# Query and key score stacks: high and low parts made for both heads at once, the other row halves moved by DMA

## The chip, the cores and the metric

The kernel runs on one core of a Trainium2 chip. The metric is the device time of one execution in microseconds. A core has TensorE (PE; PEld is its weight load), VectorE (DVE), ScalarE (ACT), GpSimd (POOL) and SyncE (SP), which issues this kernel's DMAs from one queue, in order.

## The reference, cut to what matters

Two decoder layers run one after the other on 1024 positions of width 1024, in float32. Layer 0 mixes tokens by differential attention (8 heads of two 64-wide queries and keys, with a rotary embedding on 16 of the 64), layer 1 by forgetting attention (16 heads of 64). Each is followed by a layer norm and a gated MLP with a causal convolution.

```
q, k, v = jnp.split(x @ w_qkv, 3, axis=-1)
q = apply_rotary(q.reshape(B, S, H, 2, d), cos, sin, PARTIAL_ROT)...
s = jnp.einsum('bhcqd,bhckd->bhcqk', qb, k) * scale
p = masked_softmax(s, causal_mask(start, Q_BLOCK, S))
a = (p[:, :, 0] - lam * p[:, :, 1]).astype(v.dtype)
o = jnp.einsum('bhqk,bhkd->bqhd', a, v)
...
s = (jnp.einsum('bhqd,bhkd->bhqk', qb, k).astype(jnp.float32) * scale
     + cb[..., :, None] - c[..., None, :])
```

## The kernel before, in words

Float32 products are made of parts. `split` (L84 to L91) makes a high part in fp32r on ScalarE (L87) and the rest, the low part, on VectorE (L89, or L91 where a scale is applied). `mm3` (L98 to L100) multiplies high by high, low by high and high by low.

Sixteen head halves (layer 0) or heads (layer 1) are worked on in 8 pairs. A pair's projections are transposed: 128 rows are the features, 64 of each head, and 1024 columns are positions, made in two halves `c` of 512. For the scores each head has a stack of 128 rows. A query stack holds the high part in one half of its rows and the low part in the other: stack a has head 0's high part in rows 0 to 63 and its low part below, stack b head 1's high part in rows 64 to 127 and its low part above. A key stack holds the high part twice, and a third tile holds the low parts of both heads' keys. `scores` (L475 to L491) multiplies the stacks (L489), adds the query's high part, copied by GpSimd into `qz` (L482), times the keys' low part (L490), and the mask (L491).

`split_q` makes a site of 64 rows twice: two high and two low parts for a pair's half. `split_k` makes, for each head, a high part, a low part and a copy of the high part on ScalarE (L275). In layer 1 `result` (L409) calls them on the projection in PSUM. In layer 0 the projection is copied to a tile by L414, the rotary comes between, and `halves` (L420) calls them on the tile. The rotary is `gather` (L428: twelve small DMAs for a half, L437 and L439), `turn` (three VectorE operations, L446 to L448, and four DMAs back, L452).

`project` makes the next pair's projections in steps of a few matmuls, which are put between the attention jobs of the pair at work; `after` puts the eviction, the gathers, the turn and the halves a set number of steps behind the matmuls (D_EV, D_ROT, D_CUT). Within these, a scheduler sets the order of instructions on each engine. A softmax row block goes: scores on TensorE, maximum (L510), exponential (L513, ScalarE), reciprocal (L516), division (L518) or the difference of the two maps (L523), transposes on TensorE (L1304), their high and low parts `pt` (L87, L89), products with V. V is transposed by L458 and its parts are `q<-m` of 128 x 512. Weights are fetched on SP (L107, tag `wst`, 2 buffers, which the second map's exponential also takes) and split into `wh` and `wl`.

Of the kernel before, what the change touches and what calls it, by code (L numbers as in the profile page):

```python
# [9 lines left out]
F32 = mybir.dt.float32  # L10
F32R = mybir.dt.float32r
BF16 = mybir.dt.bfloat16
I32 = mybir.dt.int32
AF = mybir.ActivationFunctionType
# [5 lines left out]
P = 128  # L20
# [6 lines left out]
DH = 64  # L27
# [27 lines left out]
class Trunk:  # L55
# [205 lines left out]
    def qtile(self, par):  # L261
        return self.qp.tile([P, 1024], F32R, tag=f"q{par}", name=self.nm("q"))

    def split_q(self, par, src, scale, sl):

        for st, r in zip(par, (0, 64)):
            self.split(st[r:r + 64, sl], st[64 - r:128 - r, sl], src[r:r + 64, :], scale)

    def split_k(self, par, src, sl):

        a, b, lo = par
        for st, r in ((a, 0), (b, 64)):
            s = src[r:r + 64, :]
            self.split(st[r:r + 64, sl], lo[r:r + 64, sl], s)
            self.nc.scalar.activation(st[64 - r:128 - r, sl], s, AF.Copy)  # L275


    def after(self, n, fn, *args):
# [131 lines left out]
    def result(self, l, s, c, ps, dst, t):  # L410

        sl = slice(c * 512, c * 512 + 512)
        if dst is not None:
            self.nc.scalar.activation(dst[:, sl], ps, AF.Copy, scale=DH ** -0.5 if s == 0 else 1.0)  # L414
        elif s == 0:
            self.split_q(t[:2], ps, -DH ** -0.5, sl)
        else:
            self.split_k(t[2:5], ps, sl)

    def halves(self, dst, t, c, j):  # L420

        sl = slice(c * 512, c * 512 + 512)
        if j == 0:
            self.split_q(t[:2], dst[0][:, sl], None, sl)
        else:
            self.split_k(t[2:5], dst[1][:, sl], sl)

# [1082 lines left out]
```

## Time and profile before

| | us |
|---|---|
| three runs | 2513.72, 2516.26 (median), 2519.29 |
| profiled execution | 2511.37 |
| its span | 2509.6 |
| TensorE busy in the span | 2445.9 |
| VectorE busy | 1956.6 |
| ScalarE busy | 1336.5 |
| attention of layer 0, pairs 0 to 7 | about 45 to 500 |
| attention of layer 1 | about 1297 to 1740 |

Times in the trace count from the start of the span. Columns of a timeline are the start, the duration, the engine, the line, the operation, output and input, and in brackets the engine's idle time before it with what ended it. The duration of a matmul is modelled and pipelined, so that starts, not durations, tell how far apart matmuls are.

### The profile page before, as it was taken

Reading aid. Unit: us, or ns where it says so; the run is one execution under the profiler, and the core shown is the slowest. Engines: PE = TensorE matmul, PEld = TensorE weight load, DVE = VectorE, ACT = ScalarE, POOL = GpSimd, SP = SyncE. Lnnn points to the kernel's source line nnn. Section 1 sums busy time; section 2 is a strip of 40 time slices with the busy share of each in tenths; the row PEclk is TensorE's granted clock in tenths of the full one; section 3 lists DMA queues with packets and bytes.
Section 4 is the critical chain, followed back from the end, with each engine's and each line's share of the span. In section 5 each row is a group of like instructions: output and inputs, shape, how many; then the busy total and the mean of one; then the engine's idle time right before and its main releaser. Section 6 shows DMA issues by size and latency. Waiting matters only on the chain.

```text
span 2509.6 us, 33808 instructions
## 1 busy us (share of the span) xinstructions
PE 2445.9 (97%) x12059; PEld 2017.6 (80%) x12059; DVE 1956.6 (78%) x3669; ACT 1336.5 (53%) x2519; POOL 140.1 (6%) x322
## 2 busy tenths in 40 slices
PE   8999999999999999999999999999999999999997
PEld 6888777787888888788778888888878888888786
DVE  6787777989876677787868888888888667677867
ACT  5666666656544444444545666656465444444444
POOL 2001101101000000000101000000010000000001
PEclk9999999999999999999999999999999999999999
DMA  4111111422222223864411111114222222228743
GB/s 153 39 57 56 47 47 48 175 93 92 93 82 95 76 76 132 312 199 155 148 54 51 51 51 51 51 60 160 84 85 101 84 76 81 96 97 286 241 138 140
DMA packets 101865, 264.32 MB, mean 105 GB/s; under 512 B 15008, under 2 KB 22560, under 8 KB 101696
## 3 DMA queue, kind: packets, MB, share of 16 engines
q1 hardware_dynamic: 101184, 261.31, 30.5%
q8 instruction: 94, 1.54, 0.3%
q0 software_dynamic: 512, 0.85, 0.1%
q14 instruction: 75, 0.61, 0.1%
HBM read 196.70 MB, written 59.11 MB: 102 GB/s over the span
## 4 chain that ended last, share of the span: by engine, by line
PE 49%; DVE 5%; DMA 2%; ACT 1%; issue 1%; SPq 0%; POOL 0%; POOLq 0%; DVEq 0%; ACTq 0%
PE m L98 11%; PE m L100 11%; PE m L99 11%; PE s L100 3%; PE s L98 3%; PE s L99 3%; PE m L1304 2%; PE m L1329 1%; PE m L1330 1%; PE s L490 1%; PE s L489 1%; DMA ha<-ad 1%; DVE wo L89 1%; DVE wl L89 0%; DVE s L635 0%
## 5 line engine op out<-in xcount | busy, mean ns | idle before, releaser
L98 PE MATMUL m<-xh,wh 128*128 128x512 f32 x768 | 322.3, 420 | 9.1 <-ACT xh L87 8.8
L100 PE MATMUL m<-xh,wl 128*128 128x512 f32 x768 | 304.2, 396 | 0.0
L99 PE MATMUL m<-xl,wh 128*128 128x512 f32 x768 | 302.2, 393 | 0.4 <-DVE xl L89 0.4
L98 PE MATMUL m<-xh,wo 128*128 128x512 f32 x656 | 255.2, 389 | 0.0
L100 PE MATMUL m<-xh,wo 128*128 128x512 f32 x656 | 255.2, 389 | 0.0
L99 PE MATMUL m<-xl,wo 128*128 128x512 f32 x656 | 255.2, 389 | 0.0
L87 ACT ACTIVATE wo<-wg 128x512 fp32r<-128x512 f32 x168 | 106.4, 633 | 225.6 <-PE m L100 218.6
L87 ACT ACTIVATE pt<-m 128x512 fp32r<-128x512 f32 (+1 forms) x240 | 128.4, 552 | 121.1 <-PE m L1304 83.6
L98 PE MATMUL m<-q,wo 128*128 128x512 f32 x472 | 184.1, 390 | 0.0
L99 PE MATMUL m<-q,wo 128*128 128x512 f32 x472 | 183.8, 389 | 0.0
L100 PE MATMUL m<-q,wo 128*128 128x512 f32 x472 | 183.7, 389 | 0.0
L98 PEld LDWEIGHTS m<-xh,wh 128*128 128x128 f32 x768 | 145.7, 190 | 32.4 <-ACT xh L87 8.8
L100 PEld LDWEIGHTS m<-xh,wl 128*128 128x128 f32 x768 | 144.8, 188 | 31.5 <-DVE wl L89 0.6
L89 DVE TENSOR_TENSOR pt<-m,pt 128x512 fp32r<-128x512 f32 (+1 forms) x240 | 149.0, 632 | 22.5 <-ACT pt L87 19.8
L99 PEld LDWEIGHTS m<-xl,wh 128*128 128x128 f32 x768 | 145.7, 190 | 23.6 <-DVE xl L89 0.9
L87 ACT ACTIVATE wo<-t 128x512 fp32r<-128x512 f32 x132 | 82.8, 627 | 144.7 <-PE m L100 133.3
L89 DVE TENSOR_TENSOR wo<-wg,wo 128x512 fp32r<-128x512 f32 x168 | 115.4, 688 | 38.8 <-ACT wo L87 37.9
L482 POOL CAST qz<-q 64x128 fp32r<-64x128 f32 x256 | 93.3, 365 | 911.2 <-PE s L491 831.4
L98 PEld LDWEIGHTS m<-xh,wo 128*128 128x128 f32 x656 | 123.1, 188 | 25.7 <-ACT p L1037 0.2
L100 PEld LDWEIGHTS m<-xh,wo 128*128 128x128 f32 x656 | 123.1, 188 | 25.6
L99 PEld LDWEIGHTS m<-xl,wo 128*128 128x128 f32 x656 | 123.2, 188 | 25.4
L87 ACT ACTIVATE oa<-ha 128x512 fp32r<-128x512 f32 x108 | 67.4, 628 | 127.4 <-PE s L100 61.1
(319 smaller groups left out, 6363.5 us busy)
## 6 DMA issues: line engine op xcount, KB each, us to landing
wst<-in_w SPq DMA_DIRECT2D x46, 512.0 KB, 3.3
t<-in_wi SPq DMA_DIRECT2D x44, 512.0 KB, 4.4
ad<-t SPq DMA_DIRECT2D x44, 512.0 KB, 3.4
ha<-ad SPq DMA_DIRECT2D x88, 256.0 KB, 5.4
wg<-in_wi SPq DMA_DIRECT2D x42, 512.0 KB, 3.3
pt<-in_wd SPq DMA_DIRECT2D x34, 512.0 KB, 3.5
wb<-in_wd SPq DMA_DIRECT2D x42, 256.0 KB, 3.0
wst<-in_wo SPq DMA_DIRECT2D x16, 512.0 KB, 3.3
```

The costliest lines, as they stand in the source:

```text
L87: nc.scalar.activation(hi, src, AF.Copy, scale=1.0 if scale is None else scale)
L89: nc.vector.tensor_tensor(lo, src, hi.bitcast(F32), op=ALU.subtract)
L98: mm(out, wh, xh, start=start, stop=False)
L99: mm(out, wh, xl, start=False, stop=False)
L100: mm(out, wl, xh, start=False, stop=stop)
L482: nc.gpsimd.tensor_copy(qz[r:r + 64, :], q[r:r + 64, qt * P:qt * P + P])
L489: nc.tensor.matmul(sb[:, ks], q[:, qt * P:qt * P + P], kd[:, ks], start=True, stop=False)
L490: nc.tensor.matmul(sb[:, ks], qz, kl[:, ks], start=False, stop=not last)
L1304: nc.tensor.transpose(tb[:, w:w + P], self.pts[q][:, kt * P:kt * P + P], k.ident)
L1329: mm(o, self.v[0][:, vs], h, start=first, stop=False)
L1330: mm(o, self.v[0][:, vs], l, start=False, stop=last)
```

## The change

`split_q` and `split_k` work on all 128 rows, so that there is one high part and one low part for both heads. The halves of rows that then stand in the wrong stack are moved by `move`: three DMAs of 64 x 512 (128 KB) on SP for a query and three for a key, at 32 sites each. For a query: the high part of head 1 to stack b, the low part of head 1 to b's upper rows, then the low part of head 0 over the rows of a that held head 1's high part (which waits for the first move). For a key: the high part of head 1 to b, twice, then the high part of head 0 over a's lower rows (which waits for both). The low part of a query is written over the source tile in layer 0, and into a new tile `ql` (tag `t`) in layer 1. Lines behind the edit move by 4 or 6: L414 is L418, L437 to L439 are L443 to L445, L452 is L458, L458 is L464, L510 to L523 are L516 to L529, L1304 is L1310; the moves are L266.

```
+    def move(self, *pairs):
+        for dst, src in pairs:
+            self.nc.sync.dma_start(dst.bitcast(F32), src.bitcast(F32))
+
+    def split_q(self, par, src, scale, sl, lo):
+        a, b = par[0][:, sl], par[1][:, sl]
+        self.split(a, lo, src, scale)
+        self.move((b[64:], a[64:]), (b[:64], lo[64:]), (a[64:], lo[:64]))
...
-        for st, r in zip(par, (0, 64)):
-            self.split(st[r:r + 64, sl], st[64 - r:128 - r, sl], src[r:r + 64, :], scale)
...
-        a, b, lo = par
-        for st, r in ((a, 0), (b, 64)):
-            s = src[r:r + 64, :]
-            self.split(st[r:r + 64, sl], lo[r:r + 64, sl], s)
-            self.nc.scalar.activation(st[64 - r:128 - r, sl], s, AF.Copy)
+        a, b = par[0][:, sl], par[1][:, sl]
+        self.split(a, par[2][:, sl], src)
+        self.move((b[64:], a[64:]), (b[:64], a[64:]), (a[64:], a[:64]))
...
         elif s == 0:
-            self.split_q(t[:2], ps, -DH ** -0.5, sl)
+            if c == 0:
+                self.qlo = self.tp.tile([P, 1024], F32R, tag="t", name=self.nm("ql"))
+            self.split_q(t[:2], ps, -DH ** -0.5, sl, self.qlo[:, sl])
...
         if j == 0:
-            self.split_q(t[:2], dst[0][:, sl], None, sl)
+            self.split_q(t[:2], dst[0][:, sl], None, sl, dst[0][:, sl].bitcast(F32R))
```

The scheduler puts the instructions into a new order around this. On SP, at the start of pair 0 (t_144 and t_145 are its query and key, t_382 the rotary's tile, q_137 and q_138 the query stacks, q_139 and q_140 the key stacks), there stood before, from the last gathers of the second half on:

```order
L437 DMA t_382<-t_145 32x256
L439 DMA t_382<-t_145 16x256 x2
L107 DMA wst_562<-in_w 128x1024
L564 DMA bf<-in_bf 16x1
L568 DMA tri<-in_tri 128x128
L452 DMA t_144<-t_382 32x256 x2
L452 DMA t_145<-t_382 32x256 x2
L107 DMA wst_673<-in_w 128x1024
```

and now, from the last moves of the first half on:

```order
L266 DMA q_140<-q_139 64x512
L266 DMA q_137<-t_144 64x512
L445 DMA t_382<-t_144 16x256
L443 DMA t_382<-t_145 32x256
L266 DMA q_139<-q_139 64x512
L445 DMA t_382<-t_145 16x256 x2
L443 DMA t_382<-t_145 32x256
L445 DMA t_382<-t_145 16x256 x2
L107 DMA wst_562<-in_w 128x1024
L570 DMA bf<-in_bf 16x1
L574 DMA tri<-in_tri 128x128
L458 DMA t_144<-t_382 32x256 x2
```

So the first half's moves stand among the gathers of the second half, and the rotary's way back (L458, before L452) behind them all.

On ScalarE, in the second half of a middle pair (the one at 278 us; q_2469 to q_2472 are the next pair's stacks, pt_3161 a transposed probability), there stood before:

```order
L87 ACTIVATE q_2469<-t_2679 64x512
L87 ACTIVATE q_2470<-t_2679 64x512
L87 ACTIVATE q_2471<-t_2781 64x512
L87 ACTIVATE pt_3161<-m_3111 128x384
L275 ACTIVATE q_2471<-t_2781 64x512
L513 ACTIVATE wst_3167,ls_3093<-s_3086,nm_3092 128x1024
```

and now:

```order
L552 ACTIVATE sq_2967<-sq_2967 128x256
L87 ACTIVATE q_2469<-t_2679 128x512
L87 ACTIVATE pt_3161<-m_3111 128x384
L87 ACTIVATE q_2471<-t_2781 128x512
L519 ACTIVATE wst_3167,ls_3093<-s_3086,nm_3092 128x1024
```

The high part of `pt` stood behind the key's half and stands ahead of it now.

On VectorE, at the boundary of pair 0 and pair 1 (q_564 and q_565 are pair 1's query stacks, q_568 the low part of its keys), there stood before:

```order
L89 TENSOR_TENSOR pt_1148<-m_1109,pt_1148 128x384
L89 TENSOR_TENSOR q_565<-t_672,q_565 64x512
L89 TENSOR_TENSOR q_568<-t_760,q_566 64x512
L510 TENSOR_REDUCE nm_1139<-s_1135 128x1
L516 RECIPROCAL rs_1189<-ls_1091 128x1
L89 TENSOR_TENSOR q_568<-t_760,q_567 64x512
L522 TENSOR_TENSOR rs_1189<-rs_1189,nlam 128x1
L516 RECIPROCAL rs_1217<-ls_1140 128x1
L523 SCALAR_TENSOR_TENSOR p_1107<-wst_1154,rs_1189,p_1107 128x1024
```

and now:

```order
L89 TENSOR_TENSOR pt_1148<-m_1109,pt_1148 128x384
L557 SCALAR_TENSOR_TENSOR of_747<-sq_960,of_747 128x256
L522 RECIPROCAL rs_1190<-ls_1091 128x1
L89 TENSOR_TENSOR q_568<-t_760,q_566 128x512
L528 TENSOR_TENSOR rs_1190<-rs_1190,nlam 128x1
L516 TENSOR_REDUCE nm_1139<-s_1135 128x1
L529 SCALAR_TENSOR_TENSOR p_1107<-wst_1154,rs_1190,p_1107 128x1024
```

One low part stands between `pt` and the difference of the maps, where three stood.

## Rows read from the trace of the kernel before

**Rows 1.** The page: busy time of each engine
```profile
PE 2445.9 (97%) x12059; PEld 2017.6 (80%) x12059; DVE 1956.6 (78%) x3669; ACT 1336.5 (53%) x2519; POOL 140.1 (6%) x322
```

**Rows 2.** Windows: length, busy time of each engine, granted clock, DMA share, GB/s
```profile
60.00:500.00 440.00, 423.26 (x2318) 350.25 (x2318) 355.57 (x720) 288.58 (x617) 43.84 (x116) 1.00 0.20 66
1310.00:1740.00 430.00, 423.84 (x2490) 354.68 (x2489) 348.34 (x841) 261.14 (x553) 37.64 (x108) 1.00 0.19 64
```

**Rows 3.** TensorE's waits, 60 to 500 us: line, releaser, total, times, longest
```profile
PE m L458 <- DVE pt L89: 10.8, 6, 2.4
...
PE m L1304 <- DVE p L523: 1.6, 1, 1.6
```

**Rows 4.** TensorE's waits, 1310 to 1740 us
```profile
PE m L1304 <- DVE q L91: 1.2, 6, 0.2
```

**Rows 5.** Timeline of TensorE at the start of pair 0
```profile
49.21 0.39 PE L489 MATMUL s<-q,q 128*128 128x256 f32 x1 [0.97 <-ACT p L513]
...
51.98 0.39 PE L100 MATMUL m<-xh,wl 128*128 128x512 f32 x1
52.21 0.40 PE L98 MATMUL m<-xh,wh 128*128 128x512 f32 x1
53.96 0.39 PE L489 MATMUL s<-q,q 128*128 128x256 f32 x1 [1.35 <-ACT wst L513]
...
57.85 0.50 PE L1304 MATMUL m<-ident,p 128*128 128x128 f32 x3
```

**Rows 6.** Groups by line and shape: count, busy us, mean ns, idle before
```profile
L89 DVE TENSOR_TENSOR q<-t,q 64x512 fp32r<-64x512 f32 x64 | 44.0, 688 | 2.1 <-ACT q L87 0.4
L87 ACT ACTIVATE q<-t 64x512 fp32r<-64x512 f32 x64 | 40.1, 627 | 3.8 <-DMA t<-t 2.7
...
L89 DVE TENSOR_TENSOR xl<-t,xh 128x512 fp32r<-128x512 f32 x32 | 21.3, 682 | 1.5 <-ACT xh L87 1.5
...
L87 ACT ACTIVATE xh<-t 128x512 fp32r<-128x512 f32 x32 | 18.7, 628 | 4.6 <-DMA t<-od 4.6
```

**Rows 7.** DMA issues: count, KB of each, median us from issue to landing
```profile
wst<-in_w SPq DMA_DIRECT2D x46, 512.0 KB, 3.3
...
t<-t SPq DMA_DIRECT2D x128, 32.0 KB, 1.8
...
out<-acc SPq DMA_DIRECT2D x3, 128.0 KB, 1.9
```

**Rows 8.** Timeline of SP's queue: issue of the rotary's way back, pair 0
```profile
46.44 2.41 SPq L452 DMA_DIRECT2D t<-t  x4
```

**Rows 9.** Timeline of VectorE at the boundary of pairs 0 and 1
```profile
101.06 1.40 DVE L89 TENSOR_TENSOR q<-t,q 64x512 fp32r<-64x512 f32 x2
...
102.76 0.81 DVE L89 TENSOR_TENSOR q<-t,q 64x512 fp32r<-64x512 f32 x1
...
103.80 1.28 DVE L523 SCALAR_TENSOR_TENSOR p<-wst,rs,p 128x1024 f32<-128x1024 f32 x1
```

**Rows 10.** Timelines of ScalarE, VectorE and TensorE around 278 us
```profile
274.87 1.28 ACT L87 ACTIVATE q<-t 64x512 fp32r<-64x512 f32 x2
277.03 0.63 ACT L87 ACTIVATE q<-t 64x512 fp32r<-64x512 f32 x1 [0.89 <-DMA t<-t]
...
275.85 1.22 DVE L510 TENSOR_REDUCE nm<-s 128x1 f32<-128x1024 f32 x1
278.07 0.56 DVE L89 TENSOR_TENSOR pt<-m,pt 128x384 fp32r<-128x384 f32 x1 [1.00 <-ACT pt L87]
...
278.68 0.66 PE L458 MATMUL m<-ident,t 128*128 128x128 f32 x4 [2.01 <-DVE pt L89]
```

**Rows 11.** Timeline of VectorE in the pairs at 217 and 400 us
```profile
216.10 1.22 DVE L510 TENSOR_REDUCE nm<-s 128x1 f32<-128x1024 f32 x1
217.46 0.56 DVE L89 TENSOR_TENSOR pt<-m,pt 128x384 fp32r<-128x384 f32 x1
...
400.30 0.56 DVE L89 TENSOR_TENSOR pt<-m,pt 128x384 fp32r<-128x384 f32 x1 [1.20 <-ACT pt L87]
```

More of the change, by code (lines that the diff above doesn't have):

```diff
@@ L262, in qtile @@
         return self.qp.tile([P, 1024], F32R, tag=f"q{par}", name=self.nm("q"))
-    def split_q(self, par, src, scale, sl):
-        for st, r in zip(par, (0, 64)):
-            self.split(st[r:r + 64, sl], st[64 - r:128 - r, sl], src[r:r + 64, :], scale)
-    def split_k(self, par, src, sl):
-        a, b, lo = par
-        for st, r in ((a, 0), (b, 64)):
-            s = src[r:r + 64, :]
-            self.split(st[r:r + 64, sl], lo[r:r + 64, sl], s)
-            self.nc.scalar.activation(st[64 - r:128 - r, sl], s, AF.Copy)
+    def move(self, *pairs):
[5 more added lines that the diff above has]
+        self.move((b[64:], a[64:]), (b[:64], lo[64:]), (a[64:], lo[:64]))
+    def split_k(self, par, src, sl):
+        a, b = par[0][:, sl], par[1][:, sl]
+        self.split(a, par[2][:, sl], src)
+        self.move((b[64:], a[64:]), (b[:64], a[64:]), (a[64:], a[:64]))
     def after(self, n, fn, *args):
```

## The prediction

> **What bounds the kernel now.** I read the page first, then the windows of the two attention stretches, then TensorE's waits in them, then the timelines of the few waits that are left. On the page TensorE is busy for 97% of the span [rows 1]; no other engine is the bound, and ScalarE and VectorE matter only where TensorE waits for them. The change touches the two attention stretches. There TensorE is idle for 440.00 - 423.26 = 16.7 us in layer 0 and 430.00 - 423.84 = 6.2 us in layer 1 [rows 2], at full clock in both. So about 23 us is all that a lighter ScalarE and VectorE could win, out of some 2516.
>
> The waits say where that is [rows 3, 4]. Six times 1.8 us on average (10.8 in all) TensorE's transposes of V (L458) wait for the low part of a transposed probability, `pt`. Once, for 1.6 us, transposes of probabilities (L1304) wait for VectorE's L523. In layer 1 it is six times 0.2 us behind the low part of a query (L91). Before these windows, at the start of the first pair, scores wait 0.97 and 1.35 us for exponentials [rows 5]. Everything else is TensorE's own work, which the change leaves as it is.
>
> **What the split costs.** An operation of 64 rows takes as long as one of 128: the low part of 64 x 512 takes 688 ns, of 128 x 512 682; the high part 627 and 628 [rows 6]. So in layer 0 VectorE's 64 low parts of 44.0 us become 32 of 21.8, and ScalarE's 64 high parts of 40.1 us, with 32 copies of the same size beside them, become 32 of 20.1. Layer 1 has as many sites. These are large cuts, and nearly all of it is cover: TensorE waits for neither engine except at the places above. The work goes, the time doesn't, unless one of those waits ends earlier.
>
> **What the moves cost.** Each of the 64 sites issues three transfers of 128 KB on SP: 192 more, 25 MB. None like them is in the trace. From below, a 32 KB transfer between the same kind of tiles lands in 1.8 us; from above, 512 KB of weights land in 3.3; the nearest row is a 128 KB store with 1.9, and I take that [rows 7]. Issuing holds SP for 2.41 / 4 = 0.6 us each [rows 8]. The third transfer of a site waits for earlier ones to land (it overwrites what one of them reads), so a stack is whole about 0.6 x 3 + 1.9 + 1.9 = 5.6 us after its parts exist. In the middle pairs and in layer 1 the scores that read the stack come later than that, since the halves are made while the pair before is still at work; there the moves alone cost nothing. What they hold up is SP's queue: rotary gathers, the rotary's way back (L452) and weight fetches stand behind them, in order.
>
> The Trainium skill, in "SBUF — State Buffer", section "The DMA setup-cost knee (why "@ 1 MiB" ≠ asymptote)", gives a transfer a fixed 2 us and a rate on top, and advises 128 partitions and few, large transfers, which speaks against 192 moves of 64 partitions; its fit makes one of 128 KB 2.3 us, as an estimate. The 1.8 and 1.9 of the rows agree with a fixed part that is most of it, and are smaller. By 2.3 the third move of a site at the start would come 0.4 later and the term below would be -0.1 in place of -0.5; the rest stays hidden.
>
> **Term 1, the start of pair 0: -0.5 us.** Two waits, 0.97 + 1.35 = 2.3 us [rows 5], come from ScalarE's twelve 64-row halves standing ahead of the exponentials. Now four stand there, and the second two go behind the exponentials; I replay only 0.2 of the 2.3 left. But the first site's six moves stand among the gathers of the second half, and the rotary's way back, issued at 46.44 now [rows 8], has six issues (3.6 us) and a landing ahead of it: I put it at 50.5, its fourth transfer at 52.9 with the landing at 54.7. ScalarE's half waits in order until then, and the exponential behind the halves starts at about 56.5. VectorE needs its two low parts (0.68 each), a maximum and L523 before the probabilities are ready, about 58.7. TensorE, 2.3 us ahead, would want the transposes that stand at 57.85 now [rows 5] at 57.0, since they now stand behind six matmuls of 0.23 us (the spacing of the rows at 51.98 and 52.21). So 1.7 is paid back of 2.1 and some 0.4 to 0.5 is kept. Ends: -2.3 (no payback), and +1.7 (the payback on top of no gain).
>
> **Term 2, the boundary of pair 0 and 1: -1.4 us.** Ahead of L523 at 103.80 stand three low parts, 1.40 + 0.81 us [rows 9]; one of 0.68 is left, so L523 ends 1.5 earlier, and TensorE's 1.6 us [rows 3] falls to about 0.2. Ends: -1.6 and 0 (a wait for the half's landing takes its place).
>
> **Term 3, V's transposes: -1.7 us.** In the pair at 278 ScalarE's `pt` stands behind the high part of a key, which waits for the rotary's transfer (0.89), and VectorE's `pt` waits 1.00 for it [rows 10]. In the new order `pt` stands ahead of the key's half: it could go at 274.87 + 0.63. VectorE's maximum ends at 275.85 + 1.22 = 277.07, and `pt` can follow 0.14 later, as in the pair at 217, where VectorE sets it already [rows 10, 11]. So it starts at 277.2, not 278.07: 0.87 off this pair's wait of 2.01. The pair at 400 shows the same pattern, with 1.20 [rows 11]; twice 0.87 is 1.7. In the other four the low part follows the maximum, and the move of ScalarE's instruction does nothing. Ends: 0, and -10.8 if all six waits go.
>
> **Term 4, layer 1: -1.0 us.** The L91 that frees TensorE's bank was two of 64 rows and is one; that is more than the 0.2 missing, six times [rows 4]. Ends: -1.2 and 0. Layer 1's moves stand behind weight fetches, but a pair's stacks have a whole pair's time.
>
> **Term 5, VectorE's chain: +1.0 us.** In the first half of a middle pair the new order puts a weight's high part behind V's copy from PSUM and its low part behind the division of 896 columns, so the chain up to the maximum and `pt` ends later: I estimate 0.25 us in each of the four pairs that VectorE bounds. Ends: 0 and four low parts of 0.68, 2.7.
>
> Sum: -0.5 - 1.4 - 1.7 - 1.0 + 1.0 = -3.6 us. The profiled execution took 2511.37, 4.9 less than the median of the three runs, 2516.26; so 2507.8 beside the former and **2512.7** beside the latter. A measurement can tell about 0.2%, 5.0 us, from no change.
>
> **The rivals.**
> *A, relief throughout.* If `pt`'s low part is late because VectorE carries 64-row low parts earlier in the pair, all six waits of L458 go, and with them the start's, the boundary's and layer 1's: 10.8 + 2.3 + 1.6 + 1.2 = 15.9, to 2500.4. For it: VectorE is busy for 355.57 of 440 us there [rows 2] and loses 22. Against it: in four of six pairs what stands just ahead of `pt` is a maximum of 1.22 us that itself waits for scores, not a half.
> *B, slower: the way back of the rotary, late.* What I find at the start, moves among the gathers of the second half, stands in every middle pair too. If the six moves and the landing they wait for make L452 late there, ScalarE waits in order at the half with the exponential behind it, and the payback of 1.7 us comes six times, while term 3 goes: -3.6 + 10.2 + 1.7 = +8.3, to 2524.6. For it: the key's half already waits 0.89 for that transfer [rows 10], so nothing is in reserve there. Against it: I find the gathers only some 0.5 us later, because the queue idles between pairs of them, and VectorE reaches its rotary later than they land. It decides when the gathers slip by more than that.
> *C, nothing.* VectorE's sequence from scores to maximum to exponential re-forms the waits elsewhere: 2516.3. For it: TensorE is at 97%.
> That the change does not do what it says can be left out: 128 fewer ScalarE and 64 fewer VectorE instructions stand in the order, 192 more transfers on SP, and as many matmuls as before.
>
> **How the numbers follow.** The forecast case has 0.45, with a range of its own of 2508 to 2517 (start and V's transposes between half and double); A 0.20, B 0.20, C 0.15. Faster by over 0.2%: A, and the 0.17 of the forecast that lies below 2511.3: 0.37. Slower: B, and 0.02 of C: 0.22. Within: the rest, 0.41. The range goes to 2501 and 2525, which leaves out about half of A and half of B, 0.2 in all.
>
> **What would show it.** Right: the waits of 0.97 and 1.35 at the start gone, with one of 1 to 2 us at L1310 (now L1304) near 57; the 1.6 at 105 down to a few tenths; two of the six waits of V's transposes shorter by about 0.9 and four unchanged; layer 1's six gone; moves landing in about 1.9 us. Wrong: V's waits gone in all six pairs (A), or ScalarE's halves waiting over 1 us for the rotary's transfers in the middle pairs (B), or a first score of a pair that waits for a move.

## The result, and the profile after

The changed kernel takes 2492.6 us (median of four runs, 2488.05 to 2495.28) beside 2514.99 of the kernel before: a ratio of 0.9906, 95% interval 0.9892 to 0.992. Run again beside the last experiments it was 0.9902 [0.9888, 0.9916]. That is 22 to 24 us faster where 3.6 were forecast, and below the range. The profiled execution spans 2493.5 us, 16.1 less than the one before. The profiled execution before lay 3.6 us below the median of those runs and the one after 2.7 above the median of its own, which is the rest.

First the busy times on the page, then the windows of the attention of layer 0 and layer 1, which answer to [rows 1, 2]:

```profile
PE 2439.9 (98%) x12059; PEld 2017.0 (81%) x12059; DVE 1908.1 (77%) x3605; ACT 1260.3 (51%) x2391; POOL 138.4 (6%) x322
```

```profile
60.00:485.00 425.00, 418.68 (x2319) 348.31 (x2318) 334.09 (x696) 255.44 (x564) 40.67 (x117) 1.00 0.32 96
1293.00:1723.00 430.00, 425.29 (x2516) 359.74 (x2515) 333.17 (x823) 231.18 (x505) 40.96 (x109) 1.00 0.29 87
```

ScalarE is busy for 76 us less and VectorE for 48; the counts of the prediction make about 80 and 44. TensorE is idle for 425.00 - 418.68 = 6.3 us in layer 0, where it was 16.7; in layer 1 for 4.7, where it was 6.2. TensorE's waits in layer 0, which answer to [rows 3]:

```profile
PE m L464 <- DVE pt L89: 2.2, 4, 1.1
PE m L548 <- ACT sq L544: 2.0, 6, 0.3
PE m L98 <- DVE pt L89: 0.9, 1, 0.9
PE m L1310 <- DVE sq L556: 0.6, 1, 0.6
PE m L464 <- DVE sq L556: 0.4, 1, 0.4
```

The waits of V's transposes are 2.6 us in place of 10.8, and the 1.6 at the boundary of pairs 0 and 1 is gone. The moves, in the list of DMA issues, take longer than the 1.9 us that were assumed:

```profile
q<-q SPq DMA_DIRECT2D x128, 128.0 KB, 2.3
...
q<-t SPq DMA_DIRECT2D x32, 128.0 KB, 2.4
q<-ql SPq DMA_DIRECT2D x32, 128.0 KB, 3.1
```

To see where the time went I took the start of V's transposes as marks. Three of them, in TensorE's timeline before:

```profile
46.64 0.28 PE L458 MATMUL m<-ident,t 128*128 128x128 f32 x1
...
116.30 0.38 PE L458 MATMUL m<-ident,t 128*128 128x128 f32 x2
...
463.17 0.44 PE L458 MATMUL m<-ident,t 128*128 128x128 f32 x2 [1.80 <-DVE pt L89]
```

and the same three after:

```profile
48.34 0.49 PE L464 MATMUL m<-ident,t 128*128 128x128 f32 x3
...
113.93 0.49 PE L464 MATMUL m<-ident,t 128*128 128x128 f32 x3
...
447.88 0.44 PE L464 MATMUL m<-ident,t 128*128 128x128 f32 x2 [0.20 <-DVE pt L89]
```

"Start" is the stretch from the first mark to the second (pair 0 and its boundary), "middle pairs" from the second to the third. "Layer 1" is taken in the same way from the last transpose ahead of it to the first behind it: before from 1261.3 to 1835.1, after from 1245.4 to 1813.7. The table has the length of each stretch against the kernel before for all runs; kernels are described below. A negative number is time won.

| kernel | ratio (95%) | start 69.66 | middle 346.87 | layer 1 573.8 |
|---|---|---|---|---|
| changed | 0.9906 (0.9892 to 0.992) | -4.1 | -12.9 | -5.5 |
| the same again (e11) | 0.9902 (0.9888 to 0.9916) | -3.1 | -15.2 | -5.6 |
| layer 0 alone (e1) | 0.9923 (0.9907 to 0.9939) | -3.8 | -14.4 | -0.6 |
| layer 1 alone (e2) | 0.9988 (0.9978 to 0.9998) | 0.0 | -1.0 | +0.6 |
| low parts by 64 rows (e3) | 0.9958 (0.9942 to 0.9973) | -0.1 | -9.4 | -4.0 |
| high parts by 64 rows (e4) | 0.994 (0.9922 to 0.9958) | -2.0 | -12.3 | -5.9 |
| keys only (e5) | 0.9963 (0.995 to 0.9976) | -3.3 | -4.7 | -3.5 |
| before, fetch earlier (e6) | 0.9964 (0.9952 to 0.9977) | -1.2 | -7.7 | +0.6 |
| moves twice (e7) | 0.9959 (0.9946 to 0.9972) | +3.4 | -14.1 | -4.3 |
| changed, fetch earlier (e8) | 0.9926 (0.9911 to 0.994) | -3.2 | -12.8 | -4.4 |
| gathers first (e9) | 0.9939 (0.9925 to 0.9953) | +0.2 | -13.0 | -1.5 |
| moves on GpSimd (e10) | 0.9983 (0.9974 to 0.9992) | +0.2 | -3.3 | -7.3 |
| GpSimd, gathers first (e12) | 0.9983 (0.9973 to 0.9993) | -1.0 | -2.0 | -6.8 |
| GpSimd, fetch earlier (e13) | 0.9939 (0.9922 to 0.9956) | -1.3 | -10.6 | -7.9 |
| layer 0 SP, layer 1 GpSimd (e14) | 0.989 (0.9875 to 0.9905) | -3.8 | -15.0 | -8.0 |

The stretches come from one execution each and don't add up to the ratio: what lies between V's last transposes of layer 0 and layer 1 (the end of the last pair, the output projection and the first MLP) goes from -1.2 to +7.3 us against the kernel before. The two executions of the changed kernel show 2.3 us of difference in the middle pairs.

Part of the spread is TensorE's clock. In each execution its granted clock (the 0.50 in the windows below; 1.00 is full) falls for some stretches of 3.4 to 14 us to its lower level, 1.2 in place of 2.4 GHz. One in e7 and one in e2:

```profile
58.10:64.90 6.80, 6.16 (x16) 4.39 (x17) 5.05 (x11) 3.31 (x9) 0.60 (x2) 0.50 0.55 148
```

```profile
1302.60:1312.80 10.20, 8.49 (x26) 5.77 (x25) 6.30 (x22) 5.04 (x13) 0.66 (x3) 0.50 0.33 90
```

Matmuls of 512 columns then start 0.43 us apart in place of 0.23, so that 3.4 us at the lower level can cost some 1.6 us (an estimate from these spacings). Of the middle pairs only e12's hold such a stretch (3.4 us). In "start" e7 has 6.8 us of it, and e3, e9 and e10 have 3.4. In "layer 1" e2 has 13.7, e9 10.2, and the kernel before, e1, e5, e6, e7, e8 and e12 have 3.4; the changed kernel, e11 and the others have none. So differences between the rows in "start" and "layer 1" are in part the clock's.

**Where the middle pairs won.** A pair's first half, before the change, on ScalarE:

```profile
258.86 0.90 ACT L513 ACTIVATE wst<-s,nm 128x768 f32<-128x768 f32 x1
...
262.95 1.06 ACT L87 ACTIVATE wh<-wst 128x1024 fp32r<-128x1024 f32 x1 [1.09 <-DMA wst<-in_w]
263.92 0.58 ACT L414 ACTIVATE t<-m 128x512 f32<-128x512 f32 x1
264.39 1.00 ACT L513 ACTIVATE p<-s,nm 128x896 f32<-128x896 f32 x1
```

and the same place after:

```profile
251.90 0.89 ACT L519 ACTIVATE wst<-s,nm 128x768 f32<-128x768 f32 x1
...
256.16 1.01 ACT L519 ACTIVATE p<-s,nm 128x896 f32<-128x896 f32 x1
...
257.46 0.59 ACT L418 ACTIVATE t<-m 128x512 f32<-128x512 f32 x1
257.94 1.06 ACT L87 ACTIVATE wh<-wst 128x1024 fp32r<-128x1024 f32 x1
```

Before, the exponential of 896 columns stood behind a weight's high part, which waited for its fetch, and behind V's copy. It started 5.5 us behind the exponential of 768 columns. Now it stands ahead of both and starts 4.3 behind it; counted from the last V transposes (235.37 before, 230.50 after), 29.0 became 25.7. So it is 3.4 us earlier in the pair. Not all of this is ScalarE's order. The maximum that this exponential needs, before and after:

```profile
262.06 1.09 DVE L510 TENSOR_REDUCE nm<-s 128x1 f32<-128x896 f32 x1
```

```profile
255.03 1.09 DVE L516 TENSOR_REDUCE nm<-s 128x1 f32<-128x896 f32 x1
```

It starts 26.69 behind the mark before and 24.53 after, 2.2 earlier; ahead of it VectorE now has two low parts of 128 rows where it had four of 64. The other 1.2 are the order on ScalarE: the exponential starts 2.3 behind this maximum before and 1.1 after. VectorE's division, the next maximum and `pt` follow from the exponential. The second maximum of 896 columns, before and after:

```profile
266.32 1.08 DVE L510 TENSOR_REDUCE nm<-s 128x1 f32<-128x896 f32 x1
```

```profile
260.17 1.08 DVE L516 TENSOR_REDUCE nm<-s 128x1 f32<-128x896 f32 x1
```

It is 30.95 us behind the mark before, 29.67 after: 1.3 earlier.

### The profile page after: what moved, and what is told of

It is laid out like the page before. It is cut to its first block, busy times and chain, and to the rows that moved or that the text cites. A ratio compares the mean times of both kernels' runs of the same rounds, so it can differ in the third digit from the quotient of the medians.

```text
span 2493.5 us, 34031 instructions
## 1 busy us (share of the span) xinstructions
PE 2439.9 (98%) x12059; PEld 2017.0 (81%) x12059; DVE 1908.1 (77%) x3605; ACT 1260.3 (51%) x2391; POOL 138.4 (6%) x322
## 5 line engine op out<-in xcount | busy, mean ns | idle before, releaser
L495 PE MATMUL s<-q,q 128*128 128x512 f32 (+3 forms) x384 | 130.6, 340 | 2.1 <-ACT p L649 1.8
```

The lines of the kernel that those rows point to most:

```text
L495: nc.tensor.matmul(sb[:, ks], q[:, qt * P:qt * P + P], kd[:, ks], start=True, stop=False)
```

## The experiments

Four explanations were set against each other: VectorE's load (fewer low parts), ScalarE's load (fewer high parts and copies), the new order on ScalarE around the second weight, and the cost of the moves.

**e1 and e2: one layer at a time.** `split_q` and `split_k` take the new form in one layer, the old one in the other. In e1, for the keys (e2 asks for layer 1):

```
+        if self.lay == 0:
+            a, b = par[0][:, sl], par[1][:, sl]
+            self.split(a, par[2][:, sl], src)
+            self.move((b[64:], a[64:]), (b[:64], a[64:]), (a[64:], a[:64]))
+            return
+        a, b, lo = par
...
```

> The change in layer 0 alone; layer 1 as before. If the gain sits in the layer 0 attention (the two traces differ by 15.0 us at its end), this keeps about 15 us: ratio 0.993 to 0.995. If layer 1 or a change that runs on through both layers carries most of it, 5 us or less: 0.998 to 1.000. Layer 1's six waits of L1304 for L91 are back.

> The change in layer 1 alone. The two traces differ there by some 4.5 to 6 us, 0.65 us in each middle pair: ratio 0.997 to 0.998, and the six waits of V's transposes in layer 0 are 10.8 us as before. If the gains of the layers are independent, this and the kernel with layer 0 alone add up to the whole (0.991).

2495.72 and 2513.54 us, beside 2515.88: 20 and 2.3 us won, together the whole. Layer 0 carries it; it won more than the 15 us expected, and layer 1 less than its 4.5 to 6. Layer 1's stretch in e2 shows no gain (+0.6 against -5.5), though five of its middle pairs take 313.2 us (V's transposes from 1374.38 to 1687.60) as in the changed kernel (1349.60 to 1662.82), where the kernel before takes 316.6 (1367.88 to 1684.45). The start of the layer lost what these pairs won: TensorE's scores there wait 3.2 us for exponentials (1.8 in the changed kernel), and behind these waits its clock is at the lower level for the 10.2 us shown above.

**e3 and e4: the loads, each put back.** The changed kernel with each low part (e3, shown without its scaled form), or each high part (e4), made by two operations of 64 rows:

```
+        for r in (0, 64):
+            l, s, h = lo[r:r + 64], src[r:r + 64], hi[r:r + 64].bitcast(F32)
+            if scale is None:
+                nc.vector.tensor_tensor(l, s, h, op=ALU.subtract)
...
```

> Changed kernel, but each low part of a site made by two VectorE operations of 64 rows (64 more VectorE operations, 44 us, as before the change); ScalarE and the moves as changed. Theory of VectorE's load: its chain of maxima is late again, V's transposes wait again about 8 to 11 us, and of some 22 us gained 10 or more are lost: ratio 0.995 to 0.998. Theory of order (the exponential of 896 columns ahead of the weight's high part and V's copy on ScalarE, which this kernel keeps): at most 4 us are lost, ratio 0.990 to 0.9925, V's transposes wait under 4 us.

> Changed kernel, but each high part of a site made by two ScalarE operations of 64 rows (64 more ScalarE operations, about 39 us, half of what the change took away); VectorE and the moves as changed. Theory of ScalarE's load: about half of the gain is lost, ratio 0.995 to 0.997. Theories of VectorE's load and of order: within 4 us of the changed kernel, 0.990 to 0.9925.

e3 took 2504.69, which loses half of the gain: as the theory of VectorE's load has it by its ratio. But where it loses is not as that theory has it. The start loses all of its 4 us, 3.2 of them at the boundary of pairs 0 and 1, where TensorE waits 1.6 us for VectorE and then runs for 3.4 us at the lower clock. The middle pairs lose only 3.5 of 12.9, and V's transposes wait little:

```profile
PE m L475 <- DVE pt L89: 1.9, 2, 1.1
```

So with VectorE's old load and the new order the middle pairs keep 9.4 us. The maximum shown above stands 24.9 behind the mark here, so that its 2.2 us don't come from the load by itself either. e4 took 2498.34 (0.994, between the two expectations) and keeps 12.3 of 12.9 in the middle pairs. What it loses lies at the start, and behind the third mark: up to V's next transposes 3.6 us of what was won go again. ScalarE's load by itself is not what the middle pairs won by.

**e5 and e6: the order.** e5 leaves the queries as before and changes the keys alone. This takes away 96 of 128 ScalarE instructions, but the scheduler leaves the weight's high part and V's copy ahead of the exponential. e6 is the kernel before, with the second weight fetch of a pair one projection earlier in layer 0:

```
-                if n in (1, 4):
-                    self.ahead(i + 2 + n // 4)
+                if n in (1, 3):
+                    self.ahead(i + 2 + n // 3)
```

> Only the keys' parts made of 128 rows with three moves; the queries as before. It takes away 96 of the 128 ScalarE and 32 of the 64 VectorE instructions, but the order keeps the weight's high part and V's copy ahead of the exponential of 896 columns, as before the change. If the engines' load alone set the gain, half or more is kept: ratio 0.993 to 0.9955. If the order around that exponential carries much of it, V's transposes still wait 6 us or more and the ratio is 0.996 to 0.999.

> The kernel before, every split of 64 rows, no moves; in layer 0 the second weight fetch of a pair stands one projection earlier (after the third one, not the fourth), so that ScalarE's order has the exponential of 896 columns ahead of the weight's high part, as the change has. Theory of order: layer 0 wins 6 to 12 us without any change of the splits, ratio 0.995 to 0.9976, V's transposes wait under 6 us. Theory of the engines' load alone: 0.999 to 1.001, and the waits of 10.8 us stay.

e5 took 2505.8 (0.9963), as the theory of order had it: the middle pairs win 4.7, and V's transposes wait 8.1 us, now mostly for another operation of VectorE:

```profile
PE m L461 <- DVE sq L553: 6.6, 5, 2.0
...
PE m L461 <- DVE pt L89: 1.5, 1, 1.5
```

e6 took 2504.34 (0.9964, 9.7 us won) with every operation of 64 rows still there. The middle pairs win 7.7. The exponential goes first there:

```profile
256.64 0.90 ACT L513 ACTIVATE wst<-s,nm 128x768 f32<-128x768 f32 x1
...
259.85 1.01 ACT L513 ACTIVATE p<-s,nm 128x896 f32<-128x896 f32 x1 [0.21 <-DVE nm L510]
...
260.85 0.59 ACT L414 ACTIVATE t<-m 128x512 f32<-128x512 f32 x1
```

V's transposes still wait 8.1 us, more than expected. The rest of what e6 won stood in waits that the waits view does not name (see below).

**e7: the moves twice.**

```
         for dst, src in pairs:
-            self.nc.sync.dma_start(dst.bitcast(F32), src.bitcast(F32))
+            for _ in range(2):
+                self.nc.sync.dma_start(dst.bitcast(F32), src.bitcast(F32))
```

> Changed kernel with each move issued twice (192 more transfers of 128 KB, on the same queue); order on ScalarE and VectorE unchanged in the middle pairs. If the moves are covered but for the start of pair 0 and the rotary's way back, it costs up to 6 us over the changed kernel, ratio 0.991 to 0.993. If SP's queue is near the path everywhere (the way back of the rotary later by 1.8 us or more in each pair), 10 us or more: 0.9945 and above.

2502.91 (0.9959), 10 to 12 us over the changed kernel, which is the second expectation by its ratio. By place it is the first: the start takes 7.5 us more (+3.4 in place of -4.1), the middle pairs on balance nothing (-14.1). At the start TensorE waits 0.78 and 1.21 us for exponentials, and then its clock is at the lower level for the 6.8 us shown above, which by the spacing of the matmuls is some 3 of the 7.5 us. The profiled execution (2511.30) is the slowest of the eight and spans 16.0 us more than the changed kernel's. Of the rest, 3.9 us lie between the third mark and V's next transposes, and 6.6 in the output projection and the first MLP, where its clock is at the lower level for 6.8 us and the changed kernel's for none. Beyond that I have no cause for it.

**e8: the change and the earlier fetch together.**

> Changed kernel with the earlier fetch of the kernel above. If the change had already won what the earlier fetch wins, within 4 us of the changed kernel: 0.990 to 0.9925. If the two add up, 0.986 to 0.989.

2494.86 (0.9926, interval to 0.994): 2 to 4 us over the changed kernel by medians, with intervals that overlap, and the middle pairs win 12.8. What e6 wins, the change had won already; the two don't add up.

**e9, e10, e12: the order of the moves.** e9 issues the gathers of pair 0's second half ahead of the first half's moves, by putting the whole of the first half's splits behind them; e10 issues all moves from GpSimd's queue; e12 does both. e9, then e10:

```
-                self.halves(dst, t, 0, 0)
-                self.halves(dst, t, 0, 1)
...
             self.gather(dst, r, c)
+            if c:
+                self.halves(dst, t, 0, 0)
+                self.halves(dst, t, 0, 1)
```

```
-            self.nc.sync.dma_start(dst.bitcast(F32), src.bitcast(F32))
+            self.nc.gpsimd.dma_start(dst.bitcast(F32), src.bitcast(F32))
```

> Changed kernel, but at the start of pair 0 the gathers of the second half are issued ahead of the moves of the first half. If those moves among the gathers cost time there (doubling them cost 6.2 us at that place), this wins 1 to 3 us over the changed kernel: ratio 0.989 to 0.9905 where that one has 0.9906. If the first scores, which wait for the moves, take their place: as the changed kernel or up to 3 us slower, 0.991 to 0.992.

> Changed kernel with all moves issued from GpSimd's queue in place of SP's. If it is SP's order that the moves cost (rotary and weights behind them), 2 to 5 us faster than the changed kernel: 0.9885 to 0.99. If GpSimd's issue or its copies of the query behind the waiting moves come to stand on the path, slower than the changed kernel by 3 us or more: 0.992 and above.

> The changed kernel once more, for the comparison with the runs beside it: 0.9906 plus or minus 0.0015.

> Both: moves on GpSimd's queue and the gathers first at the start. If the gathers first help only by clearing SP's queue, as with GpSimd's queue alone, within 2 us of it. If the two help at different places, 1 to 3 us below the better one.

e9 lost more than either expectation allowed: 2498.51, the start at +0.2. The first scores wait 0.88 us for a move, and ScalarE has both 128-row halves, which wait for the rotary, ahead of the first exponential:

```profile
53.83 0.63 ACT L87 ACTIVATE q<-t 128x512 fp32r<-128x512 f32 x1 [1.26 <-DMA t<-t]
54.37 0.35 ACT L520 ACTIVATE p<-s,nm 128x128 f32<-128x128 f32 x1
```

A projection then waits 1.59 us for a weight's high part (at 57.69), and from 58.0 TensorE's clock is at the lower level for 3.4 us. The edit moves splits as well as gathers, so it doesn't price the order of the queue alone. Its stretch of layer 1, whose code is the changed kernel's, shows -1.5 only, with 10.2 us at the lower clock.

e10 lost nearly everything: 2510.74, with all low and high parts of 128 rows and SP's queue clear of moves. The middle pairs win 3.3. The scheduler had put the weight's high part ahead of the exponential again:

```profile
256.77 0.89 ACT L519 ACTIVATE wst<-s,nm 128x768 f32<-128x768 f32 x1
...
262.36 1.06 ACT L87 ACTIVATE wh<-wst 128x1024 fp32r<-128x1024 f32 x1 [4.09 <-DMA wst<-in_w]
...
263.58 1.02 ACT L519 ACTIVATE p<-s,nm 128x896 f32<-128x896 f32 x1
```

Here the exponential is 6.8 us behind that of 768 columns, and 3.6 behind its maximum (which is as early as in the changed kernel, 24.6 behind the mark). e12 is the same (2510.44); the gathers first don't matter there. e11, the changed kernel beside them, took 2490.58, as expected. Layer 1 wins 7.3 in e10, more than with SP.

**e13: is it GpSimd or the order?** The moves on GpSimd's queue, with the earlier fetch of e6:

> Moves on GpSimd's queue, and the second weight fetch of a pair one projection earlier in layer 0. With GpSimd's queue alone ScalarE's order has the weight's high part, which waits 4.09 us for the fetch, ahead of the exponential of 896 columns, and layer 0's gain is gone. If it is that order and wait, the earlier fetch brings most of the gain back: ratio 0.989 to 0.993, V's transposes wait under 4 us. If it is GpSimd's issuing or its copies behind waiting moves, the kernel stays at 0.9965 to 0.999.

2500.37 (0.9939), a little over the first expectation: the middle pairs go from 3.3 to 10.6 us won, though 192 moves are still issued by GpSimd. V's transposes wait 5.5 us where under 4 were expected, so it is not all of it; what the remaining 2 to 5 us of the middle pairs are was not tried. Behind the third mark, up to V's next transposes, the kernels with all moves on GpSimd take 4 to 5 us more than the kernel before (the changed one 0.8 to 1.4 less), which is most of what e13 still lacks. TensorE waits there once for 3.9 to 4.2 us for VectorE; why was not tried.

**The middle pairs in two parts.** Long stretches run from a pair's second transposes of V to the next pair's first (six, 260.96 us before), and hold the exponential above; short ones from the first to the second (five, 85.91). Against the kernel before:

| kernel | long | short |
|---|---|---|
| changed; again (e11) | -9.8; -12.3 | -3.2; -2.9 |
| low parts by 64 rows (e3) | -10.0 | +0.6 |
| high parts by 64 rows (e4) | -9.2 | -3.2 |
| keys only (e5) | -5.5 | +0.7 |
| before, fetch earlier (e6) | -5.5 | -2.2 |
| moves on GpSimd (e10) | -0.3 | -2.9 |
| GpSimd, fetch earlier (e13) | -8.3 | -2.3 |

The long stretches' gain goes with the late exponential (e10) and comes back with the earlier fetch (e13); VectorE's old load (e3) takes nothing from it. The short ones' gain goes with the low parts of 64 rows (e3) and stays without the order (e10). The order alone (e6) is worth 5.5 us in the long stretches, about half, and 2.2 in the short ones, and e5 wins as much there with the exponential still late. So the rest of the long stretches' gain comes from order and load together, and these runs don't tell them apart.

**e14: each layer with the better queue.**

> Changed kernel with the moves of layer 1 alone on GpSimd's queue, those of layer 0 on SP's. Layer 1's attention took 7.3 us less than before with GpSimd's queue and 5.4 to 5.6 with SP's: if the places are independent, 1 to 2 us below the changed kernel, 0.989 to 0.990; if not, as it, 0.9900 to 0.9915.

2488.74 (0.989, interval 0.9875 to 0.9905): the fastest kernel here, layer 1 at -8.0 and layer 0 as with the change. It beats the kernel before clearly. Over the changed kernel it is 2 to 4 us by medians, with intervals that overlap.

## Why the prediction was wrong, point by point

By place, start and boundary (terms 1 and 2) were forecast at -1.9 us and show -4.1 and -3.1; the middle pairs (terms 3 and 5) at -0.7 and show -12.9 and -15.2; layer 1 (term 4) at -1.0 and shows -5.5.

**The bound and the counts** were right: the work went about as counted, TensorE bounds the kernel, and doubling layer 0's moves cost time at the start and not in the middle pairs (e7).

**Term 1 (start, -0.5) and term 2 (boundary, -1.4)** had the right signs and places: both waits of [rows 5] and the 1.6 of [rows 3] are gone. But only the second wait of [rows 5] came from halves. The exponential behind the first (0.97 us) stood on ScalarE behind a weight's high part, which waited for its fetch, though its maximum had ended at 46.61:

```profile
47.76 1.06 ACT L87 ACTIVATE wh<-wst 128x1024 fp32r<-128x1024 f32 x1 [2.00 <-DMA wst<-in_w]
48.72 0.35 ACT L513 ACTIVATE p<-s,nm 128x128 f32<-128x128 f32 x1
```

Now it stands ahead of that high part, as in the middle pairs:

```profile
50.28 0.36 ACT L519 ACTIVATE p<-s,nm 128x128 f32<-128x128 f32 x1
...
53.99 1.06 ACT L87 ACTIVATE wh<-wst 128x1024 fp32r<-128x1024 f32 x1 [0.39 <-DMA wst<-in_w]
```

The payback of 1.7 us did not come: no wait stands near 57. I let ScalarE's first half wait for the rotary's fourth transfer. The query's half waits only for the two that write the query: the four transfers were issued from 52.87 to 55.60, and the half started at 55.48, in an execution whose first copies of the projections (L414, now L418) came 2.0 us later, at 35.61 in place of 33.60.

**Term 5 (+1.0, no gain allowed) is the step that failed.** It saw the new order, and took the weight's high part, now behind V's copy L414, for a delay of VectorE's chain, as if V's copy could not start before 263.92. The copy had no wait of its own; it stood in ScalarE's order behind the high part that waited for its fetch, and the exponential of 896 columns behind both. The term left this exponential out. After the change V's copy starts at 257.46 without a wait, 26.96 us behind the mark, where it was 28.55. The chain is 1.3 us earlier in that pair, not 0.25 later, and e6 shows the price of that order by itself: 7.7 us in the middle pairs.

**Term 3 (-1.7)** rested on four pairs in which the low part follows a maximum, and held that VectorE sets them. That is so, but the maximum itself comes earlier by the 1.3 above. So those pairs gained as well, and the waits fell from 10.8 to 2.6. The gain from `pt` standing ahead of the key's half is there in part: ScalarE's query half now waits for the rotary (1.26 us at 270.09), and VectorE's `pt` waits 0.21 for it in place of 1.00.

**The waits were too small a measure.** 23 us were taken as all that could be won. That 22 to 24 were won is chance: TensorE's idle time in the two windows fell by only 10.4 and 1.5 us. Term 4 went by layer 1's 1.2 us of waits behind L91. The middle pairs of layer 1 became shorter by 0.68 us each (V's transposes from 1360.60 to 1423.91 before, from 1342.76 to 1405.39 after), 3.4 in five. At a place where such a wait stood, the matmul before stood at 1363.02 and the transposes at 1363.62:

```profile
1363.02 0.40 PE L99 MATMUL m<-xl,wh 128*128 128x512 f32 x1
1363.62 0.52 PE L1304 MATMUL m<-ident,p 128*128 128x128 f32 x3 [0.20 <-DVE q L91]
```

That is 0.60 apart where TensorE's pace there is 0.23: 0.37 lost, of which the view shows 0.20, since a matmul's modelled end covers the rest. What else layer 1 won, some 2 us, lies at its start, where the kernel before has 3.4 us at the lower clock (from 1297.5) and the changed kernel none. In layer 0 it is the same: from V's transposes at 218.08 to the next at 235.37 are 17.29 us, after the change 16.50, without a wait of over 0.2 in the list.

**The moves** landed in 2.3 to 3.1 us, not 1.9. What they cost shows at the start (e7). By the fit in the Trainium skill, "SBUF — State Buffer", section "The DMA setup-cost knee (why "@ 1 MiB" ≠ asymptote)", 128 KB take 2.3 us, as an estimate; the rows agree for the moves between stacks (2.3) and not for those from `ql` (3.1).

**The rivals.** A (relief throughout, 2500.4) named the right sign and the waits that went, but put it all on VectorE's load, which e3 prices at 3.5 of 12.9 us in the middle pairs and 4 at the start, a part of it the clock's; and it too counted only shown waits. Of B the sign came and the loss did not. In the changed kernel ScalarE's halves wait for the rotary's transfers nine times in layer 0, 6.6 us in all and over 1 us at 154, 270 and 447 (three times and 2.7 us before), but the middle pairs won all the same; the rotary's way back waits on SP mostly for VectorE, as it did before.

## What to carry to other kernels

In an in-order engine an instruction that starts without a wait may stand behind one that waits: before calling it released late, look for the instruction ahead of it, and for when its input was ready. Where a scheduler sets the order, price the order by itself; here one fetch, issued one projection earlier, gave 0.36% without touching the splits that the change was about. And compare start-to-start distances of matmuls, not only the listed waits, with the granted clock of each stretch beside them.

## What was not expected

The same 192 moves left layer 0's gain in place on SP, which also carries gathers and weights, and took it away on GpSimd (0.9983): the queue of a transfer changed the order that the scheduler gave ScalarE, and with the fetch earlier (e13) most of the gain was back. A weight's fetch in that place waited 4.09 us on ScalarE. Layer 1 did the opposite: in the executions without a stretch at the lower clock it won 7.3 to 8.0 us with GpSimd's queue (e10, e13, e14) against 5.5 and 5.6 with SP's; why was not tried.
